# A side-by-side input projection with pre-scaled operands and a shorter weight lead, in a two-layer trunk kernel

## The chip, the cores and the metric

The kernel runs on one core of a Trainium2 chip. The metric is the time of one launch in device microseconds (us). A core has engines that run side by side, each through its own list of instructions in order: TensorE (PE; its weight loads are shown as PEld), VectorE (DVE), ScalarE (ACT), GpSimd (POOL) and SyncE (SP, which issues the large transfers).

## The reference

A trunk of two layers over 256 tokens of width 2048: a Mamba-2 mixer and an FFN, then an attention mixer and an FFN. The change touches only the input of the first mixer:

```python
h = rms_norm(x, mix_norm[layer])
proj = h @ w_in
z = proj[..., :SSM_D_INNER]
xbc = proj[..., SSM_D_INNER:SSM_D_INNER + SSM_CONV_DIM]
dt_raw = proj[..., SSM_D_INNER + SSM_CONV_DIM:]
xbc = jax.nn.silu(causal_depthwise_conv(xbc, conv_w, conv_b))
...
y = ssd_chunked(xs * dt[..., None], dt * a, b_in, c_in)
y = y + xs * d_skip[:, None]
y = y.reshape(bsz, seq, SSM_D_INNER) * jax.nn.silu(z)
y = rms_norm(y.reshape(bsz, seq, SSM_N_GROUPS, group), norm_w.reshape(SSM_N_GROUPS, group))
```

`w_in` has 4096 columns of z, 4096 of x, 1024 each of B and C and 64 of dt, all float32.

## The kernel before

All weights lie in HBM as one list of 128x2048 tiles in the order of use. Each tile is loaded by SyncE into one of three buffers `w` and used as two halves of 128x1024. For each half `split` (L145) issues a ScalarE cast to a high part `wh` and a VectorE subtraction that leaves the low part `wl`. Activations, too, are kept as a high and a low part, one beside the other in an operand of a `slot`. A product is the sum of high times high, high times low and low times high. `next_half` (L160) keeps the splits ahead of TensorE by `AHEAD` halves, and `wh` and `wl` have one buffer more than that, so a split waits until TensorE has freed the buffer of an earlier half.

There are two schemes for the three products. `t_units` (L222) makes them with three matmuls of 256 columns (L240). `p_unit` (L250) makes the two that share the high weights with one matmul of 512 columns (L261: high and low operand side by side, into two halves of a bank) and the third with one of 256 (L265); the two halves of the bank have to be added afterwards (`joined`, L270). The FFNs and half of the output projections use `p_unit`; the input projection uses `t_unit`, for each of 8 groups `g` one unit of 256 columns (B and C), one of 512 (x) and one of 512 (z), and in group 0 one of 128 (dt). That is 20 halves in a group, and 2 of dt.

A unit sums in one of two accumulators `acc`. `begin_unit` (L199) lets a unit start only when the sums of the unit before the last have been read (the key `("evac", u)` is done).

Everything else is background: generators in queues, which put out one step at each `yield`. After each half `bg.step()` goes through the queues and takes one step of each, as long as the work put out, counted in estimated us of VectorE and ScalarE, leaves a debt under 0.75 of a half's `SHARE` (1.3 and 1.4). `bg.need(key)` takes steps of all queues, whatever the debt, until the key is done:

```python
    def step(self, free=False):
        self.debt = [max(d - s, -1.4) for d, s in zip(self.debt, self.SHARE)]
        for q in self.queues:
            if free or all(d < 0.75 * s for d, s in zip(self.debt, self.SHARE)):
                self.advance(q)

    def need(self, key):
        while key not in self.done:
...
            for q in self.queues:
                self.advance(q)
```

The operand of the input projection is x times its gain, without the norm's factor `rb` (a row over the tokens), which needs sums over all of x (`prep`, L377). The factor is multiplied into the sums as they are read (`scaled`, L392). After that a group's B, C and x go through a convolution (`first_tap` on ScalarE, three `taps` on VectorE), a tanh and a `gate`; `ssd` (L532) makes the group's scan with decay rows fetched by GpSimd's queue, and `ssd_norm` (L610) the operand of the output projection.

## Time and profile before

| | |
|---|---|
| median of 3 runs | 2698.09 us (2697.56 to 2698.7) |
| the profiled execution, its own time | 2698.51 us |
| its span, first to last instruction | 2696.4 us |
| TensorE busy | 2673.5 us (99%) |
| VectorE busy | 1700.7 us (63%) |
| ScalarE busy | 1326.3 us (49%) |
| mean granted TensorE clock | 0.999 |

The input projection runs from about 11 to about 550 us, the output projection follows, the first FFN is from about 700 to 1380 us, the attention layer follows, and the second FFN ends the program. A busy share says little by itself here: what counts is what TensorE waits for, and where.

### The profile page before, as it was taken

What the parts mean: (1) busy time and instruction counts of PE and PEld (TensorE: products, weight loads), DVE (VectorE), ACT (ScalarE), POOL (GpSimd) and SP (SyncE); (2) the same over time, 40 slices, a digit from 0 to 9 for tenths busy, and PEclk for the clock granted to TensorE, in tenths of its full rate; (3) what the DMA queues carried; (4) which work ended last, traced back from release to release, by engine and by line L of the source; (5) the groups of instructions that cost most, each with busy time, mean ns of one, the idle gap of its engine ahead of it and who ended that gap; (6) DMA issues with size and microseconds to landing.
All of it is one profiled execution on the core that took longest, in us unless ns stands there. A gap on an engine that the chain in (4) does not pass through costs nothing.

```text
span 2696.4 us, 40315 instructions
## 1 busy us (share of the span) xinstructions
PE 2673.5 (99%) x16460; PEld 2391.9 (89%) x16460; DVE 1700.7 (63%) x2104; ACT 1326.3 (49%) x1947; POOL 199.8 (7%) x215
## 2 busy tenths in 40 slices
PE   7999999999999999999999999999999999999999
PEld 7999999999888888888888888888888888888888
DVE  6777777756566666665555777766666666665444
ACT  5666666654454444444444555544454444444332
POOL 1011111110000000000001330220000000000000
PEclk9999999999999999999999999999999999999999
DMA  5454555545555555555555554553455555555553
GB/s 222 178 184 175 187 179 189 177 177 187 188 188 188 188 188 187 189 189 193 190 189 203 183 186 152 185 185 141 156 188 188 188 188 188 188 188 194 197 198 128
DMA packets 71432, 495.75 MB, mean 184 GB/s; under 512 B 8320, under 2 KB 8704, under 8 KB 13008
## 3 DMA queue, kind: packets, MB, share of 16 engines
q1 hardware_dynamic: 68400, 483.81, 49.5%
q0 software_dynamic: 2848, 9.37, 1.1%
q8 instruction: 129, 2.11, 0.3%
q14 instruction: 55, 0.45, 0.1%
HBM read 490.99 MB, written 2.16 MB: 183 GB/s over the span
## 4 chain that ended last, share of the span: by engine, by line
PE 98%; ACT 1%; issue 0%; DVE 0%; POOL 0%; DMA 0%; SPq 0%; ACTq 0%; POOLq 0%
PE acc L261 39%; PE acc L240 21%; PE acc L265 20%; PE acc L217 15%; PE bg L588 1%; PE bg L754 0%; PE bg L787 0%; PE bg L860 0%; PE bg L549 0%; ACT wh L38 0%; ACT slot L38 0%; PE bg L324 0%; PE bg L784 0%; PE bg L862 0%; DMA xres<-in_x_dram 0%
## 5 line engine op out<-in xcount | busy, mean ns | idle before, releaser
L38 DVE TENSOR_TENSOR wl<-w,wh 128x1024 fp32r<-128x1024 f32 x914 | 1128.3, 1236 | 904.7 <-ACT wh L38 903.7
L38 ACT CAST wh<-w 128x1024 fp32r<-128x1024 f32 x914 | 955.5, 1047 | 1089.8 <-PE acc L261 507.2
L261 PE MATMUL acc<-slot,wh 128*128 128x512 f32 x4416 | 1106.7, 392 | 2.1 <-DVE xres L38 1.7
L261 PEld LDWEIGHTS acc<-slot,wh 128*128 128x128 f32 x4416 | 794.2, 189 | 145.1 <-issue 2.7
L265 PEld LDWEIGHTS acc<-slot,wl 128*128 128x128 f32 x4416 | 602.4, 190 | 43.0
L265 PE MATMUL acc<-slot,wl 128*128 128x256 f32 x4416 | 615.7, 282 | 0.0
L240 PE MATMUL acc<-slot,wh 128*128 128x256 f32 x3232 | 430.1, 286 | 12.8 <-ACT wh L38 10.7
L240 PEld LDWEIGHTS acc<-slot,wh 128*128 128x128 f32 x3232 | 404.8, 193 | 19.9 <-ACT wh L38 10.8
L217 PE MATMUL acc<-wh,slot 128*128 128x512 f32 x1152 | 290.5, 394 | 0.0
L217 PEld LDWEIGHTS acc<-wh,slot 128*128 128x128 f32 x1152 | 213.7, 188 | 43.2
L240 PE MATMUL acc<-slot,wl 128*128 128x256 f32 x1616 | 226.8, 283 | 0.9 <-DVE wl L38 0.9
L240 PEld LDWEIGHTS acc<-slot,wl 128*128 128x128 f32 x1616 | 208.6, 192 | 1.1 <-DVE wl L38 1.1
L217 PE MATMUL acc<-wl,slot 128*128 128x512 f32 x576 | 154.2, 389 | 0.0
L217 PEld LDWEIGHTS acc<-wl,slot 128*128 128x128 f32 x576 | 108.1, 188 | 22.7
L38 ACT ACTIVATE tmp<-tmp 128x256 f32<-128x256 f32 (+1 forms) x104 | 46.8, 450 | 163.9 <-DVE tmp L38 163.6
L284 POOL TENSOR_TENSOR tmp<-tmp 128x256 f32<-128x256 f32 x32 | 27.6, 868 | 1022.1 <-ACT tmp L38 1017.0
L38 ACT ACTIVATE wide<-tmp,bias 128x128 f32<-128x128 f32 x192 | 62.9, 391 | 13.9 <-PE bg L588 9.4
L38 DVE SCALAR_TENSOR_TENSOR slot<-tmp,vec,slot 128x255 f32<-128x255 f32 (+1 forms) x144 | 67.6, 528 | 0.0
L38 DVE TENSOR_TENSOR tmp<-tmp 128x256 f32<-128x256 f32 x88 | 37.4, 425 | 42.6 <-ACT tmp L38 42.6
L38 DVE TENSOR_TENSOR tmp<-acc,tmp 128x512 f32<-128x512 f32 x88 | 60.1, 683 | 4.0 <-ACT tmp L38 4.0
L38 DVE TENSOR_TENSOR tmp<-tmp,rb 128x512 f32<-128x512 f32 x88 | 60.3, 686 | 0.1
L38 ACT ACTIVATE tmp<-slot 128x128 f32<-128x128 f32 (+1 forms) x136 | 52.7, 394 | 14.9 <-DVE slot L38 13.8
(131 smaller groups left out, 1191.3 us busy)
## 6 DMA issues: line engine op xcount, KB each, us to landing
w<-in_weights_dram SPq DMA_DIRECT2D x455, 1024.0 KB, 4.8
tmp<-acum POOLq DMA_DIRECT2D x32, 256.0 KB, 4.6
xres<-in_x_dram SPq DMA_DIRECT2D x4, 512.0 KB, 7.8
w<-in_weights_dram SPq DMA_DIRECT2D x4, 512.0 KB, 8.4
out_dram<-xres SPq DMA_DIRECT2D x8, 256.0 KB, 2.2
slot<-in_mask_dram POOLq DMA_DIRECT2D x1, 384.0 KB, 5.6
slot<-in_q_norm_dram POOLq DMA_DIRECT2D x1, 192.0 KB, 5.6
slot<-in_k_norm_dram POOLq DMA_DIRECT2D x1, 192.0 KB, 7.5
```

The costliest lines, as they stand in the source:

```text
L38: return call(out, *args, **kw)
L217: T.matmul(ps[tb], X[k][:, part, tb * P:(tb + 1) * P], w[:, k % 2, :], start=(k == 0 and i == 0), stop=(k == 15 and i == 2))
L240: T.matmul(pss[j][:, b, c, :], w[:, k % kk, m * P:(m + 1) * P], X[k][:, part, :], start=(k == 0 and i == 0 and c == 0), stop=(k == nk - 1 ...
L261: T.matmul(ps[:, m], h[:, k % 4, m * P:(m + 1) * P], X[k], start=(k == 0), stop=False, skip_group_check=True)
L265: T.matmul(ps[:, m, 0], l[:, k % 4, m * P:(m + 1) * P], X[k][:, 0, :], start=False, stop=(k == nk - 1), skip_group_check=True)
L284: G.tensor_tensor(sq[:, 0, :], sq[:, 0, :], sq[:, 1, :], OP.add)
L588: T.matmul(o[:, tb * P:], xdt[:, tb, q * 64:(q + 1) * 64], m[:, 256 * tb:256 + 128 * tb], start=(tb == 0 and q % 4 < 2), stop=(tb == 1), s ...
```

## The change

- `p_unit` takes the place of `t_unit` for all of the input projection but dt. The units of x and z are cut into two of 256 columns each, in the order x, z, x, z, and the weights are laid out in that order.
- From group 1 on the operand is x times gain times `rb`, made once by the new generator `normed` in queue 1 behind `prep`. Group 0 still uses the operand without `rb` and multiplies its sums.
- `total` reads the sums: a ScalarE copy of one half of the bank, a VectorE add of the other. The sums of z and of B and C go straight into their final slot. dt is copied out before `rb` is there.
- The reading of z, B and C stands in a queue of its own, number 3; there are four queues. `prep` moves from queue 0 to queue 1.
- `AHEAD` goes from 3 to 2, `wh` and `wl` from four buffers to three. `tmp` has 8 buffers, and the decay rows get a ring `rows` of 2.
- `ssd_norm` uses the slot of z for its squares.

```diff
...
     def tmp(shape, dt=F32):
-        return small.tile(shape, dt, tag="tmp", bufs=6, name=name("tmp"))
+        return small.tile(shape, dt, tag="tmp", bufs=8, name=name("tmp"))
+
+    def rows(shape):
+        return small.tile(shape, F32, tag="rows", bufs=2, name=name("rows"))
 
     def wide():
         return small.tile([P, 384], F32, tag="wide", bufs=4, name=name("wide"))
@@ -128,13 +131,13 @@
     def bg_bank():
         return psum.tile([P, 512], F32, tag="bg", bufs=4, name=name("bg"))
 
-    bg = Background(3, (V, A))
+    bg = Background(4, (V, A))
 
 
     n_tiles = weights.shape[0]
     raw_tiles, ready = {}, deque()
     state = dict(issued=0, split=0, used=0)
-    AHEAD = 3
+    AHEAD = 2
 
     def issue():
         j = state["issued"]
@@ -148,8 +151,8 @@
         while state["issued"] <= min(i // 2 + 2, n_tiles - 1):
             issue()
         t = raw_tiles[i // 2][:, (i % 2) * 1024:(i % 2 + 1) * 1024]
-        h = wpool.tile([P, 1024], F32R, tag="wh", bufs=4, name=name("wh"))
-        l = wpool.tile([P, 1024], F32R, tag="wl", bufs=4, name=name("wl"))
+        h = wpool.tile([P, 1024], F32R, tag="wh", bufs=3, name=name("wh"))
+        l = wpool.tile([P, 1024], F32R, tag="wl", bufs=3, name=name("wl"))
         A.copy(h, t)
         V.tensor_tensor(l, t, h.bitcast(F32), OP.subtract)
         if i % 2:
@@ -247,7 +250,7 @@
     def t_unit(ncols, X, xkey, evac, q=0):
         t_units([(0, range(16))], ncols, 16, X, xkey, [evac], q)
 
-    def p_unit(nk, X, xkey, evac):
+    def p_unit(nk, X, xkey, evac, q=0):
 
 
         u, ps = begin_unit()
@@ -264,8 +267,8 @@
                 for m in range(2):
                     T.matmul(ps[:, m, 0], l[:, k % 4, m * P:(m + 1) * P], X[k][:, 0, :], start=False,
                              stop=(k == nk - 1), skip_group_check=True)
-            bg.step()
-        bg.add(0, evac(ps, u))
+            bg.step(units[0] == 1)
+        bg.add(q, evac(ps, u))
 
     def joined(ps):
 
@@ -388,18 +391,47 @@
         V.tensor_scalar(hpar[64:128, 1:2], hpar[64:128, 1:2], -1.0, None, OP.mult)
         V.memset(hpar[0:64, 1:2], 1.0)
         bg.done.add("prep")
-
-    def scaled(sums):
-        u = tmp([P, 2, S])
-        V.tensor_tensor(u, sums, rb[:, None, :].to_broadcast([P, 2, S]), OP.mult)
-        return u
+        bg.add(1, normed())
+
+    XN = {}
+
+    def normed():
+
+        vs, ts = {}, {}
+        for j in range(10):
+            if j >= 2:
+                v, t = vs.pop(j - 2), ts.pop(j - 2)
+                V.tensor_tensor(t[:, :, 1, :], v, t[:, :, 0, :].bitcast(F32), OP.subtract)
+                store(XN, 2 * (j - 2), t)
+                bg.done.add(("XN", j - 2))
+            if 1 <= j < 9:
+                ts[j - 1] = operand()
+                A.copy(ts[j - 1][:, :, 0, :], vs[j - 1])
+            if j < 8:
+                v = vs[j] = tmp([P, 2, S])
+                for i in range(2):
+                    k = 2 * j + i
+                    V.scalar_tensor_tensor(v[:, i, :], xt[:, k, :], gains[:, k:k + 1], rb, OP.mult, OP.mult)
+            yield
+
+    def total(ps, u, g, v):
+        A.copy(v, ps[:, :, 1])
+        yield
+        V.tensor_tensor(v, ps[:, :, 0], v, OP.add)
+        bg.done.add(("evac", u))
+        if g == 0:
+            while "prep" not in bg.done:
+                yield
+            V.tensor_tensor(v, v, rb[:, None, :].to_broadcast([P, 2, S]), OP.mult)
+        yield
 
     def dt_evac(ps, u):
+        xb, e, r, q = (wide()[:, 0:S] for _ in range(4))
+        A.copy(xb, ps[:, 0, 0])
+        bg.done.add(("evac", u))
         while "prep" not in bg.done:
             yield
-        xb, e, r, q = (wide()[:, 0:S] for _ in range(4))
-        V.tensor_tensor(xb, ps[:, 0, 0], rb, OP.mult)
-        bg.done.add(("evac", u))
+        V.tensor_tensor(xb, xb, rb, OP.mult)
         A.activation(xb, xb, AF.Identity, bias=hpar[:, 0:1])
         A.activation(e, xb, AF.Abs)
         A.activation(e, e, AF.Exp, scale=-1.0)
@@ -455,78 +487,58 @@
                 V.scalar_tensor_tensor(dst[:, m, d:], u[:, m, :S - d], cwb[:, j * 48 + ct:j * 48 + ct + 1],
                                        dst[:, m, d:], OP.mult, OP.add)
 
...
     def gate(out_, th, v):
         V.scalar_tensor_tensor(out_, th, 1.0, v, OP.add, OP.mult)
 
+    def conv(u, dst, cts):
+        first_tap(u, dst, cts)
+        yield
+        taps(u, dst, cts, (2, 1))
+        yield
+        taps(u, dst, cts, (0,))
+        yield
+        A.activation(u, dst, AF.Tanh)
+        yield
+        gate(dst, u, dst)
+
     def bc_evac(g):
         def gen(ps, u):
...
+            both = slot([P, 1024])
+            bc, v = (both[:, i:i + 512].rearrange("p (a t) -> p a t", t=S) for i in (0, 512))
+            yield from total(ps, u, g, v)
+            yield from conv(v, bc, (32 + g, 40 + g))
             BC[g] = bc, both[:, 512:896]
             yield
         return gen
 
-    def x_evac(g):
+    def x_evac(g, i):
         def gen(ps, u):
...
+            v = tmp([P, 2, S])
+            yield from total(ps, u, g, v)
+            if i == 0:
+                XS[g] = slot([P, 4, S])
+            yield from conv(v, XS[g][:, 2 * i:2 * i + 2, :], (4 * g + 2 * i, 4 * g + 2 * i + 1))
+            if i == 1:
+                bg.add(2, ssd(g))
+            yield
         return gen
 
-    def z_evac(g):
+    def z_evac(g, i):
         def gen(ps, u):
...
+            if i == 0:
+                sz[g] = slot([P, 4, S])
+            z = sz[g][:, 2 * i:2 * i + 2, :]
+            yield from total(ps, u, g, z)
+            th = tmp([P, 2, S])
+            A.activation(th, z, AF.Tanh, scale=0.5)
+            yield
+            gate(z, th, z)
+            if i == 1:
+                SZ[g] = sz.pop(g)
+            yield
         return gen
 
+    sz = {}
     BC, XS, SZ, Y = {}, {}, {}, {}
 
     def ssd(g):
...
-            ac[pair] = tmp([P, 2, S])
+            ac[pair] = rows([P, 2, S])
             h = 8 * g + 2 * pair
...
-            sz = SZ[g] if b == 0 else SZ.pop(g)
+            sz = SZ[g]
...
-        bg.add(1, ssd_norm(g, xs))
-
-    def ssd_norm(g, xs):
-        sq = [tmp([P, 2, S]) for _ in range(2)]
+        bg.add(1, ssd_norm(g, xs, SZ.pop(g)))
+
+    def ssd_norm(g, xs, sq):
+        sq = [sq[:, 0:2, :], sq[:, 2:4, :]]
         for b in range(2):
             A.activation(sq[b], xs[:, 2 * b:2 * b + 2, :], AF.Square)
         yield
@@ -630,17 +642,21 @@
             store(Y, 4 * g + 2 * i, t)
             bg.done.add(("Y", 2 * g + i))
 
-    bg.add(0, prep())
+    bg.add(1, prep())
     bg.need(("XT", 1))
     for g in range(NG):
-        t_unit(256, XT, "XT", bc_evac(g))
+        X, key = (XT, "XT") if g == 0 else (XN, "XN")
+        p_unit(16, X, key, bc_evac(g), 3)
         if g == 0:
             t_unit(128, XT, "XT", dt_evac, 2)
-        t_unit(512, XT, "XT", x_evac(g))
-        t_unit(512, XT, "XT", z_evac(g))
-    bg.need("rstd")
+        for i in range(2):
+            p_unit(16, X, key, x_evac(g, i))
+            p_unit(16, X, key, z_evac(g, i), 3)
+        if g == 0:
+            XT.clear()
     bg.need(("evac", units[0] - 1))
     clear_norm()
+    XN.clear()
     t_units(OUT0, 512, 32, Y, "Y", [t_residual(nb, 32) for nb in (0, 1)])
     for pair in range(4, 8):
         p_unit(32, Y, "Y", p_residual(pair, 32))
@@ -919,8 +935,9 @@
         put(r16, (w_in, 8192 + g * P, P), (w_in, 9216 + g * P, P))
         if g == 0:
             put(r16, (w_in, 10240, 64), (w_in, 10240, 64))
-        put(r16, (w_in, 4096 + g * 512, 512))
-        put(r16, (w_in, g * 512, 512))
+        for i in range(2):
+            put(r16, (w_in, 4096 + g * 512 + i * 256, 256))
+            put(r16, (w_in, g * 512 + i * 256, 256))
 
     def put_out(w, order, nk):
         for j, ks in order:
```

The built programs show how the instructions move on an engine. Names are those of the program: `wl` the low part of a weight half, `acc` an accumulator, `bg` a bank of the background work, `wide` and `tmp` scratch, `slot` a large buffer.

VectorE in group 0, before, around the reading of x (`tmp<-acc,rb`), with the softplus steps of dt (`wide`) between:

```order
L38 TENSOR_TENSOR wl_617<-w_486,wh_616 128x1024
L38 SCALAR_TENSOR_TENSOR wide_379<-wide_379,wide_378 128x256 x2
L38 TENSOR_TENSOR wl_648<-w_486,wh_647 128x1024
L38 TENSOR_TENSOR tmp_676<-acc_384,rb 128x512
L38 SCALAR_TENSOR_TENSOR wide_379<-wide_379,wide_378 128x256 x2
L38 TENSOR_TENSOR wl_683<-w_548,wh_682 128x1024
L38 TENSOR_TENSOR tmp_712<-acc_384,rb 128x512
L38 SCALAR_TENSOR_TENSOR wide_379<-wide_379,wide_377 128x256
L38 TENSOR_SCALAR wide_376<-wide_376 128x256
L38 SCALAR_TENSOR_TENSOR wide_379<-wide_379,wide_376 128x256
L38 TENSOR_SCALAR wide_379<-wide_379,vec 128x256
L38 TENSOR_TENSOR wl_719<-w_548,wh_718 128x1024
```

The same engine after, the last rows ahead of the unit z1 of group 0; `slot_713<-acc_443` is the sum of the unit z0:

```order
L38 TENSOR_TENSOR slot_697<-tmp_685,slot_697 128x2x256
L38 SCALAR_TENSOR_TENSOR wide_333<-wide_333,wide_332 128x256 x2
L38 SCALAR_TENSOR_TENSOR slot_335<-slot_335 128x512
L38 SCALAR_TENSOR_TENSOR wide_333<-wide_333,wide_331 128x256
L38 TENSOR_SCALAR wide_330<-wide_330 128x256
L38 SCALAR_TENSOR_TENSOR wide_333<-wide_333,wide_330 128x256
L38 TENSOR_SCALAR wide_333<-wide_333,vec 128x256
L38 SCALAR_TENSOR_TENSOR slot_539<-tmp_653,slot_539 128x512
L38 TENSOR_TENSOR slot_713<-acc_443,slot_713 128x512
L38 TENSOR_TENSOR slot_713<-slot_713,rb 128x512
L38 TENSOR_TENSOR wl_725<-w_549,wh_724 128x1024
L38 TENSOR_TENSOR wl_745<-w_549,wh_744 128x1024
```

Before, a wl stands after every one to four rows; after, the rows from `wl_633` (22 rows ahead of these) to `wl_725` hold no wl, and the sum stands second to last among them.

VectorE in group 1, before, while x of group 1 is multiplied and the scan of group 0 runs (`wide`):

```order
L38 TENSOR_TENSOR wide_1235<-wide_1235,slot_449 128x384
L38 TENSOR_TENSOR wl_1281<-w_1118,wh_1280 128x1024
L38 SCALAR_TENSOR_TENSOR slot_1148<-tmp_1270,slot_1148 128x512
L38 TENSOR_TENSOR wide_1273<-wide_1273,slot_449 128x384
L38 TENSOR_TENSOR wl_1320<-w_1118,wh_1319 128x1024
L38 TENSOR_TENSOR wide_1314<-wide_1314,slot_449 128x384
L38 TENSOR_TENSOR wl_1356<-w_1197,wh_1355 128x1024
L38 TENSOR_TENSOR wide_1348<-wide_1348,slot_449 128x384
L38 TENSOR_TENSOR wl_1396<-w_1197,wh_1395 128x1024
L38 TENSOR_TENSOR tmp_1424<-acc_1082,rb 128x512
L38 TENSOR_TENSOR wide_1389<-wide_1389,slot_449 128x384
```

The same engine after, the rows ahead of the unit z1 of group 1; `slot_1295<-acc_1056` is the sum of the unit z0:

```order
L38 TENSOR_TENSOR wide_1245<-wide_1245,slot_335 128x384
L38 SCALAR_TENSOR_TENSOR slot_1043<-slot_1043,vec 128x253 x2
L38 TENSOR_TENSOR wide_1260<-wide_1260,slot_335 128x384
L38 TENSOR_TENSOR tmp_1267<-acc_1141,tmp_1267 128x512
L38 TENSOR_TENSOR wide_1270<-wide_1270,slot_335 128x384
L38 SCALAR_TENSOR_TENSOR slot_1043<-slot_1043 128x512
L38 TENSOR_TENSOR wide_1283<-wide_1283,slot_335 128x384
L38 SCALAR_TENSOR_TENSOR slot_539<-slot_539,vec,bg_1228 128x256 x2
L38 SCALAR_TENSOR_TENSOR slot_1032<-tmp_1267,vec,slot_1032 128x255 x2
L38 SCALAR_TENSOR_TENSOR slot_1032<-tmp_1267,vec,slot_1032 128x254 x2
L38 TENSOR_TENSOR slot_1295<-acc_1056,slot_1295 128x512
L38 TENSOR_TENSOR wl_1310<-w_1142,wh_1309 128x1024
```

Here too a wl stood after every one to three rows, and now none stands ahead of `wl_1310` among those shown. The last one before is `wl_1207`, the eighth in a row; six rows lie between it and the first row shown (two taps of each kind, two `wide` and a gate).

TensorE at the start, before, from the end of the dt unit to the x unit (`acc_384`); L311 and L324 are the two matmuls of the norm:

```order
L240 MATMUL acc_294<-slot_246,wl_296 128x256 x2
L240 MATMUL acc_294<-slot_251,wl_296 128x256 x2
L311 MATMUL bg_359<-ones,rb 128x2 x2
L324 MATMUL bg_367<-tmp_364,ones 128x256
L240 MATMUL acc_384<-slot_101,wh_301 128x256 x16
L240 MATMUL acc_384<-slot_101,wl_302 128x256 x8
L240 MATMUL acc_384<-slot_106,wh_329 128x256 x16
```

TensorE at the same place after (the line numbers are 3 higher; `acc_340` is the first x unit):

```order
L243 MATMUL acc_262<-slot_227,wl_264 128x256 x2
L314 MATMUL bg_327<-ones,rb 128x2 x2
L264 MATMUL acc_340<-slot_101,wh_269 128x512 x4
L264 MATMUL acc_340<-slot_106,wh_269 128x512 x4
L268 MATMUL acc_340<-slot_101,wl_270 128x256 x4
L268 MATMUL acc_340<-slot_106,wl_270 128x256 x4
L264 MATMUL acc_340<-slot_140,wh_297 128x512 x4
L264 MATMUL acc_340<-slot_145,wh_297 128x512 x4
L268 MATMUL acc_340<-slot_140,wl_298 128x256 x4
L268 MATMUL acc_340<-slot_145,wl_298 128x256 x4
L327 MATMUL bg_386<-tmp_363,ones 128x256
```

The second matmul of the norm, L324, has moved from ahead of the x unit to behind its second half.

## Rows read from the trace of the kernel before

**Rows 1.** Stretches: us from:to, length, busy us (x instructions), PEclk, DMA share, GB/s.
```profile
0.00:70.00 70.00, 53.90 (x407) 52.48 (x408) 49.06 (x77) 37.44 (x57) 9.85 (x17) 0.95 0.58 216
...
135.00:270.00 135.00, 135.00 (x1123) 131.20 (x1122) 104.21 (x152) 84.99 (x142) 23.17 (x25) 1.00 0.50 179
...
700.00:1000.00 300.00, 300.00 (x1720) 264.04 (x1719) 184.52 (x216) 142.91 (x188) 3.60 (x5) 1.00 0.52 186
```

The five busy columns are PE, PEld, DVE, ACT and POOL.

**Rows 2.** Time order of TensorE where the schemes meet: start us, us, instructions merged.
```profile
629.85 2.08 PE L240 MATMUL acc<-slot,wh 128*128 128x256 f32 x16
631.77 1.12 PE L240 MATMUL acc<-slot,wl 128*128 128x256 f32 x8
632.73 2.00 PE L261 MATMUL acc<-slot,wh 128*128 128x512 f32 x8
634.57 1.11 PE L265 MATMUL acc<-slot,wl 128*128 128x256 f32 x8
635.52 2.00 PE L261 MATMUL acc<-slot,wh 128*128 128x512 f32 x8
```

**Rows 3.** Time order of TensorE at the start; in brackets the idle time before.
```profile
31.72 0.51 PE L311 MATMUL bg<-ones,rb 128*128 128x2 f32 x4
34.57 1.22 PE L324 MATMUL bg<-tmp,ones 128*128 128x256 f32 x2 [2.35 <-POOL tmp L321]
37.56 3.75 PE L240 MATMUL acc<-slot,wh 128*128 128x256 f32 x16 [1.77 <-DVE tmp L38]
...
42.11 2.08 PE L240 MATMUL acc<-slot,wh 128*128 128x256 f32 x16
...
73.79 2.08 PE L240 MATMUL acc<-slot,wh 128*128 128x256 f32 x16
```

**Rows 4.** Time order of VectorE in the same stretch.
```profile
32.26 0.16 DVE L38 TENSOR_SCALAR rstd<-bg 128x2 f32<-128x2 f32 x1 [1.39 <-PE bg L311]
...
36.72 0.69 DVE L38 TENSOR_TENSOR tmp<-acc,rb 128x512 f32<-128x512 f32 x1
```

**Rows 5.** Stretches as in rows 1, behind the idle time of rows 3.
```profile
37.56:39.00 1.44, 1.44 (x7) 1.44 (x8) 0.18 (x1) 1.16 (x3) 0.00 (x0) 0.50 0.00 0
...
41.00:42.00 1.00, 1.00 (x10) 1.00 (x10) 1.00 (x2) 0.72 (x2) 0.00 (x0) 0.89 0.00 0
```

**Rows 6.** Time order of three engines in group 1 of the projection.
```profile
99.29 1.05 ACT L38 CAST wh<-w 128x1024 fp32r<-128x1024 f32 x1 [2.57 <-PE acc L240]
99.99 2.08 PE L240 MATMUL acc<-slot,wh 128*128 128x256 f32 x16
100.37 1.23 DVE L38 TENSOR_TENSOR wl<-w,wh 128x1024 fp32r<-128x1024 f32 x1 [0.99 <-ACT wh L38]
...
111.60 0.87 PE L588 MATMUL bg<-wide,slot 128*64 128x256 f32 x8
```

**Rows 7.** Groups of instructions: xcount, busy us, mean ns of one, idle before.
```profile
L38 DVE TENSOR_TENSOR tmp<-acc,tmp 128x512 f32<-128x512 f32 x88 | 60.1, 683 | 4.0 <-ACT tmp L38 4.0
L38 ACT COPY tmp<-acc 128x512 f32<-128x512 f32 x88 | 51.0, 580 | 5.3 <-PE acc L265 5.3
...
L38 DVE TENSOR_TENSOR wide<-wide,slot 128x384 f32<-128x384 f32 x64 | 35.2, 550 | 0.0
...
L38 DVE SCALAR_TENSOR_TENSOR slot<-tmp,vec,slot 128x254 f32<-128x254 f32 x48 | 26.5, 593 | 0.0
...
L38 DVE SCALAR_TENSOR_TENSOR slot<-tmp,vec,slot 128x253 f32<-128x253 f32 x48 | 22.3, 505 | 0.0
L38 DVE SCALAR_TENSOR_TENSOR slot<-tmp,vec,slot 128x255 f32<-128x255 f32 x48 | 21.4, 485 | 0.0
...
L38 DVE SCALAR_TENSOR_TENSOR slot<-tmp,slot 128x512 f32<-128x512 f32 x24 | 16.4, 683 | 0.0
...
L38 ACT ACTIVATE wide<-tmp,bias 128x128 f32<-128x128 f32 x192 | 62.9, 391 | 13.9 <-PE bg L588 9.4 <-DMA tmp<-acum 4.4
...
L38 DVE SCALAR_TENSOR_TENSOR wide<-wide,wide 128x256 f32<-128x256 f32 x10 | 4.2, 422 | 0.2
```

More of the change, by code (lines that the diff above doesn't have):

```diff
@@ L456, in taps @@
                                        dst[:, m, d:], OP.mult, OP.add)
-    def half_tanh(v, scale):
-        th = tmp([P, 2, S])
-        A.activation(th, v, AF.Tanh, scale=scale)
-        return th
     def gate(out_, th, v):
         V.scalar_tensor_tensor(out_, th, 1.0, v, OP.add, OP.mult)
+    def conv(u, dst, cts):
[8 more added lines that the diff above has]
+        gate(dst, u, dst)
     def bc_evac(g):
         def gen(ps, u):
-            v = scaled(ps[:, :, 0])
-            bg.done.add(("evac", u))
-            yield
-            both, cts = slot([P, 1024]), (32 + g, 40 + g)
-            bc = both[:, 0:512].rearrange("p (a t) -> p a t", t=S)
-            first_tap(v, bc, cts)
-            yield
-            taps(v, bc, cts, (2, 1))
-            yield
-            taps(v, bc, cts, (0,))
-            yield
-            th = half_tanh(bc, 1.0)
-            yield
-            gate(bc, th, bc)
+            both = slot([P, 1024])
+            bc, v = (both[:, i:i + 512].rearrange("p (a t) -> p a t", t=S) for i in (0, 512))
+            yield from total(ps, u, g, v)
+            yield from conv(v, bc, (32 + g, 40 + g))
             BC[g] = bc, both[:, 512:896]
@@ L484, in bc_evac, with gen @@
         return gen
[L486 removed]
+    def x_evac(g, i):
         def gen(ps, u):
[L488 to L495 removed]
+            v = tmp([P, 2, S])
[5 more added lines that the diff above has]
+                bg.add(2, ssd(g))
+            yield
+        return gen
+    def z_evac(g, i):
+        def gen(ps, u):
+            if i == 0:
[4 more added lines that the diff above has]
+            A.activation(th, z, AF.Tanh, scale=0.5)
             yield
[L497 to L498 removed]
+            gate(z, th, z)
+            if i == 1:
+                SZ[g] = sz.pop(g)
             yield
[L500 to L528 removed]
+        return gen
+    sz = {}
     BC, XS, SZ, Y = {}, {}, {}, {}
```

35 lines of the change are left out of this document (removed).

## The prediction

> **What bounds the kernel now.** I read the stretches first [rows 1]: TensorE is busy for the whole of the projection's stretch (135 to 270 us) and of the first FFN's (700 to 1000 us), at the full clock; the first 70 us hold 16 us of its idle time. So the time is TensorE's own list of matmuls, and whatever holds that list up. Then I read the time-ordered rows at the border of the two matmul schemes [rows 2], which give the price of the new scheme directly; then the start [rows 3, 4, 5]; then how early the split weights are ready [rows 6]; then the durations of the background steps [rows 7]. I call the work on one 128x1024 weight half a half. A half of the separate scheme is 24 matmuls of 256 columns and takes 631.77 - 629.85 + 0.96 = 2.88 us from start to start; a half of the side-by-side scheme is 8 of 512 and 8 of 256 and takes 635.52 - 632.73 = 2.79 us [rows 2].
>
> **Part 1, the matmul scheme.** The projection has 20 halves in each of 8 groups, 160 in all (the two dt halves stay as they were). They go from 2.88 to 2.79 us: 160 x 0.087 = 13.9 us off TensorE's list. VectorE and ScalarE are not on the path for this, as long as they keep up.
>
> The Trainium skill (TensorE: Matmul & The Clock Gate, section "Wait — 56ns, not 53.3ns?") puts the fixed cost of one matmul at full clock at about 2.5 ns. The side-by-side scheme saves one matmul of three at equal columns, 1280 in all, so by the page's figure the gain would be an estimated 3.2 us and the sum below 11 us higher; the trace does not agree (8 matmuls fewer make a half 0.087 us shorter, 11 ns each), and I take the trace.
>
> **Part 2, the start.** Before, the third unit (x of group 0) waits for the first unit's sums, which are multiplied by rb before their bank is free; rb needs the norm. TensorE ends L311 at 32.2 us and starts the x unit at 37.56 us, and the two matmuls between are slow [rows 3]. Then the clock stands at 0.50 until about 41 us [rows 5] and the first 16 matmuls take 3.75 us instead of 2.08, a loss of 1.7 us. After, the sums are copied and added without rb, so the x unit needs only row rstd (32.26 + 0.16 us [rows 4]) and one 128x512 add of 0.68 us behind it: it starts at about 33.2 us, 4.3 us earlier, and the clock loss should mostly go. Gain up to here 6 us.
>
> **Part 3, what is added to VectorE and ScalarE.** Per unit of 256 columns: one more ScalarE copy (0.58 us [rows 7]), and the multiplication by rb becomes an add of the same size (0.68). Once, in group 0: 16 products and 8 subtractions for the normalised operands, 16 x 0.42 + 8 x 0.68 = 12.2 us of VectorE, beside 8 casts on ScalarE. Spread out this would be hidden: VectorE has 135 - 104 = 31 us free in 135 us of the projection [rows 1].
>
> **Part 4, the order, which decides.** It is not spread out. The planner hands out background steps after each half only while its debt is under 0.75 of a half's share; `need` hands them out from all queues, whatever the debt, until the wanted step is out. The z and B/C sums now stand in a queue of their own, one whole unit behind the other, and the unit after next cannot start before its bank's sum is out. With the 12 us of normalised operands in the debt the planner gives nothing out for 8 halves, then the next `need` drains every queue at once. The built order shows it: eight wl in a row, then a run of background steps with no wl among them, the awaited add as the last but one or last. There are 12 such runs, from z1 of group 0 to z1 of group 4, each at a unit whose wanted sum is of z or B/C; from group 5 on steps and wl alternate again.
>
> What one costs: let T be the end of the half before the unit. TensorE can do nothing after T until the awaited add is done, and VectorE works its list in order. How early can it begin the run? In the trace the subtraction of a later half starts 0.38 us after a half's start and takes 1.23 us [rows 6]; the last wl ahead of the run belongs to the unit's second half, so with a lead of two it is done at T - 2.79 + 0.38 + 1.23 = T - 1.2. ScalarE is free at about T - 2.4 by the same count. So TensorE waits for the VectorE rows of the run, less 1.2 us, or for the ScalarE rows less 2.4 if these are longer.
>
> The run at z1 of group 1 (the second place shown above): 12 taps, 4 of each length, 4 x (0.485 + 0.593 + 0.505) = 6.3; 6 products of 384 at 0.55 = 3.3; 2 gates and 2 adds at 0.68 = 2.7; 2 skip terms priced as a tap, 1.0. Together 13.3 us [rows 7], a wait of 12.1. The eleven runs after the first, priced in this way: VectorE 7.2, 13.3, 5.9, 7.9, 15.1, 4.7, 9.7, 12.0, 5.9, 4.3, 6.6 us, ScalarE longer only in the tenth (8.9, mainly its 128x128 rows at 62.9/192 = 0.33 each [rows 7]). Waits: 6.0 + 12.1 + 4.7 + 6.7 + 13.9 + 3.5 + 8.5 + 10.8 + 4.7 + 6.5 + 5.4 = 82.8 us. Within a run VectorE also waits now and then for ScalarE; following the shown run step by step costs 0.45 us more, so 11 x 0.45 = 5. In these waits TensorE does the background matmuls which before stood between its halves: about 5.3 us a group (four times L588, 0.8 each [rows 6], and 2 us of smaller ones), of which 17 us fall in the waits of the four groups. 82.8 + 5 - 17 = 71 us.
>
> The first run, z1 of group 0, has 3 gates, 5 subtractions and 3 adds or products at 0.68, 12 taps (6.3), 6 operand products and 15 softplus steps at 0.42: 7.5 + 6.3 + 8.9 = 22.7 us. VectorE comes to it late: from 33.2 us TensorE needs 12 halves, to T = 67.3 us (with 0.6 for the two matmuls of the norm), and VectorE is behind. rb comes out two halves and a small matmul after 33.2, at about 39.8 us; the wl ahead of the rb work waits for the buffer of the third half, 42.2, and ends at 43.4. From there 8 wl (9.9 us) and 14.4 us of other rows, priced as above, lead up to the run, which so begins at 67.7 us. So the half after the run starts at 67.7 + 22.7 = 90.4 us. Before, that half starts at 73.79 us [rows 3]. Net loss 16.6 us, the gain of the start already in it.
>
> Each wait also lets the clock fall. In the trace 2.35 us of idle were enough for slow matmuls right behind, and the x unit then lost 1.7 us [rows 3, 5]. 12 x 1.7 = 20 us; bounds 5 (only waits over 10 us count) and 25.
>
> **Part 5, three buffers and a lead of two elsewhere.** The lead over TensorE shrinks by one half, 2.79 us: a wl is then done 1.6 us after the start of a half and needed two halves later, behind 1.85 us of the hi matmuls, about 5.8 us of slack. Outside the projection the background rows between two wl are at most about 4 us in attention and under 2 in the FFNs, where VectorE is busy 185 of 300 us [rows 1]. I price it at 0; the upper bound is a rival. The own ring for decay rows: their transfers are issued 10 us or more ahead of their first reader, 0.
>
> **The sum**, against the profiled execution of 2698.5 us (its span is 2696.4; the median of the runs is 2698.1, 0.4 lower): 2698.5 + 16.6 + 71 + 20 - 142 x 0.087 (12.4, the halves after the first run) = 2794 us. Low end with the clock at 5, no extra waits and the first run 10 us shorter: 2764. High end with the longer clock bound and 25 us of dependency waits: 2825.
>
> **Rivals.** (a) Covered runs: the awaited sum comes out early in a run, and TensorE works on its two split halves, 5.6 us, through the rest. Then each wait is shorter by 5.6: 0.4 + 6.5 + 1.1 + 8.3 + 2.9 + 5.2 + 0.9 = 25, the first 11, clock on five waits 8.5, less 12.4: 2731 us. Against it: the add stands at the end of the run. (b) The other side: VectorE and ScalarE get through the runs while TensorE is still busy, which holds if they reach each run more than 10 us ahead of T, that is if they are not held by TensorE freeing weight buffers. Then only the gains are left, 2698.5 - 13.9 - 6.0 = 2679 us, faster. For it: VectorE is free a quarter of the projection [rows 1]. Against: a subtraction starts right after a half's start [rows 6], so the lead is set by the buffers, not by VectorE. (c) The shorter lead also bites outside: 60 steps of attention with 3 us or more of VectorE between two wl cost 1 us each, 2794 + 60 = 2854 us.
>
> **How the numbers follow.** Forecast 0.78, (a) 0.07, (b) 0.08, (c) 0.07. I predict 2794 us. The range 2728 to 2840 takes in the forecast's bounds and (a), and leaves out (b) and most of (c). What this kernel's measurement can tell from no change is about 0.2%, 5 us. Faster 0.08, same 0.01, slower 0.91.
>
> **What would show it.** Right: idle time of TensorE before the side-by-side matmuls, put down to VectorE's add into a slot, in about 12 gaps between 65 and 400 us, the longest 20 us or more near 70; the granted clock at 0.5 behind them; halves of 2.79 us between; the x unit's first matmul near 33 us; nothing changed from 700 us on. Wrong: TensorE without gaps there, gaps of the length of a run less 5.6 us, or new idle time in attention and the FFNs.

## The result and the profile after

The changed kernel takes 2765.65 us, the median of 4 runs (2762.99 to 2767.5), beside 2698.39 us for the kernel before (2697.56 to 2698.85) on the same chip: 1.0249 times as long, 95% interval 1.0237 to 1.0261. That is slower by 67 us. The profiled execution took 2762.99 us (span 2761.2), 64.5 us more than that of before.

Stretches of the kernel after, with the columns of [rows 1]:

```profile
70.00:135.00 65.00, 46.09 (x258) 40.04 (x259) 42.75 (x73) 27.81 (x45) 2.42 (x4) 0.87 0.33 119
135.00:270.00 135.00, 116.95 (x635) 95.99 (x633) 84.48 (x123) 72.30 (x128) 16.91 (x19) 0.92 0.45 154
...
700.00:1000.00 300.00, 300.00 (x1722) 264.08 (x1721) 183.40 (x211) 142.12 (x182) 7.02 (x10) 1.00 0.52 187
```

TensorE, busy for all of 135 to 270 us before, is now idle for 18 of these 135 us, and the mean granted clock there is 0.92 instead of 1.00. From 700 to 1000 us TensorE is busy for the whole stretch, as in [rows 1]. Nothing is lost behind the output projection's first sums either: the first add of a sum to `xres` starts at 693.2 us (628.4 before) and the last at 2757.3 (2692.5 before), 2064.1 us later in both. What TensorE waited for in the whole program (engine, tile and line <- releaser: us in total, times, longest):

```profile
PE bg L457 <- DVE wide L38: 18.7, 1, 18.7
PE bg L600 <- DVE wide L38: 14.9, 12, 2.0
PE bg L314 <- POOL slot L628: 13.1, 3, 9.1
PE acc L264 <- ACT wh L38: 10.5, 1, 10.5
PE acc L264 <- DVE slot L38: 7.6, 6, 3.0
PE acc L264 <- DVE tmp L38: 4.9, 4, 3.3
```

The fourth row is the first weights at the start, as before. In the first three, 46.7 us, a background matmul (`bg`) waits. Only in the last two, 12.5 us, does a half of a unit wait for a sum.

TensorE at the start and at the first gap, in order of time, the answer to [rows 3]:

```profile
32.56 2.11 PE L264 MATMUL acc<-slot,wh 128*128 128x512 f32 x8
...
35.46 2.00 PE L264 MATMUL acc<-slot,wh 128*128 128x512 f32 x8
...
65.67 1.11 PE L268 MATMUL acc<-slot,wl 128*128 128x256 f32 x8
85.49 0.69 PE L457 MATMUL bg<-cm,wide 128*128 128x128 f32 x2 [18.72 <-DVE wide L38]
85.83 3.20 PE L264 MATMUL acc<-slot,wh 128*128 128x512 f32 x8
```

VectorE beside that gap:

```profile
65.88 1.22 DVE L38 TENSOR_TENSOR wl<-w,wh 128x1024 fp32r<-128x1024 f32 x1
67.02 0.69 DVE L38 SCALAR_TENSOR_TENSOR slot<-tmp,slot 128x512 f32<-128x512 f32 x1
67.62 0.69 DVE L38 TENSOR_TENSOR slot<-tmp,slot 128x512 fp32r<-128x512 f32 x1
...
73.66 1.66 DVE L38 SCALAR_TENSOR_TENSOR slot<-slot,vec 128x255 f32<-128x255 f32 x4
...
85.09 0.35 DVE L38 TENSOR_SCALAR wide<-wide,vec 128x256 f32<-128x256 f32 x1
85.36 0.68 DVE L38 SCALAR_TENSOR_TENSOR slot<-tmp,slot 128x512 f32<-128x512 f32 x1
85.96 0.68 DVE L38 TENSOR_TENSOR slot<-acc,slot 128x512 f32<-128x512 f32 x1
```

The x unit starts at 32.56 us, and its second half at 35.46 where it was 42.11 [rows 3]. TensorE ends its half at 66.6 us, VectorE begins the long run at 67.0 and ends it at 86.6. The row to look at is the last one: the add `slot<-acc` that the planner had waited for runs at 85.96, and the unit behind it in the program had begun at 85.83. TensorE waited for `wide`, written at 85.09 and read by the background matmul L457, the entry ahead of the unit in its own list. The unit itself, z1, needs only the accumulator of the unit x1: the built program gives both the same banks, and the sum of x1 was out at 70.5 us. The wanted sum, that of z0, frees the accumulator of the unit after z1.

The gap at z1 of group 1 shows the same (TensorE rows and one VectorE row, the last):

```profile
149.86 1.52 PE L600 MATMUL bg<-wide,slot 128*64 128x256 f32 x16
...
158.60 1.54 PE L600 MATMUL bg<-wide,slot 128*64 128x256 f32 x6 [0.84 <-DVE wide L38]
160.08 3.61 PE L264 MATMUL acc<-slot,wh 128*128 128x512 f32 x8
161.85 0.68 DVE L38 TENSOR_TENSOR slot<-acc,slot 128x512 f32<-128x512 f32 x1
```

TensorE goes through the run's background matmuls one by one as VectorE's products come out, and again the unit starts ahead of the add. Its first eight matmuls take 3.61 us instead of 2.00. Two stretches at this place, first the slow half, then what follows:

```profile
160.08:163.70 3.62, 3.62 (x11) 2.93 (x11) 3.59 (x5) 0.28 (x1) 0.78 (x1) 0.55 0.00 0
163.70:165.50 1.80, 1.80 (x13) 1.63 (x13) 0.70 (x1) 1.05 (x1) 0.00 (x0) 1.00 0.00 0
```

Behind 10 us in which TensorE was busy for 5.4 (150 to 160 us) the granted clock is 0.55, near the lower of its two levels, 1.2 GHz, for about a half; then it is 2.4 GHz again.

At the gap before, the unit z0 of group 1, no background matmul stands in front (one TensorE row, one VectorE row):

```profile
127.37 2.06 PE L264 MATMUL acc<-slot,wh 128*128 128x512 f32 x8 [3.25 <-DVE tmp L38]
130.30 0.69 DVE L38 TENSOR_TENSOR slot<-acc,slot 128x512 f32<-128x512 f32 x1
```

Here the unit waits for the sum of x (`tmp`), and starts 2.9 us before the awaited add. In all, nine of the twelve delayed units start before the awaited add has ended, by 0.3 to 5.6 us. The other three, at 190.46, 270.73 and 355.06 us, start 0.15 us after it.

### The profile page after: what moved, and what is told of

The parts are those of the page before. It is cut to its first block, busy times and chain, and to the rows that moved or that the text cites. A ratio compares the mean times of both kernels' runs of the same rounds, so it can differ in the third digit from the quotient of the medians.

```text
span 2761.2 us, 37728 instructions
## 1 busy us (share of the span) xinstructions
PE 2682.8 (97%) x15180; PEld 2337.1 (85%) x15180; DVE 1722.9 (62%) x2133; ACT 1350.1 (49%) x1996; POOL 203.8 (7%) x215
## 4 chain that ended last, share of the span: by engine, by line
PE 93%; DVE 3%; ACT 2%; issue 1%; DMA 0%; POOL 0%; SPq 0%; DVEq 0%; ACTq 0%; POOLq 0%
PE acc L264 48%; PE acc L268 24%; PE acc L220 14%; PE acc L243 4%; DVE slot L38 2%; DVE wl L38 1%; PE bg L600 1%; ACT wide L38 1%; ACT slot L38 0%; DVE wide L38 0%; PE bg L770 0%; PE bg L803 0%; PE bg L876 0%; ACT wh L38 0%; DVE tmp L38 0%
## 5 line engine op out<-in xcount | busy, mean ns | idle before, releaser
L264 PE MATMUL acc<-slot,wh 128*128 128x512 f32 x5696 | 1446.8, 396 | 25.6 <-ACT wh L38 10.5
L264 PEld LDWEIGHTS acc<-slot,wh 128*128 128x128 f32 x5696 | 1034.4, 191 | 219.3 <-issue 11.8
L268 PEld LDWEIGHTS acc<-slot,wl 128*128 128x128 f32 x5696 | 779.5, 191 | 56.5 <-DVE wl L38 0.3
L268 PE MATMUL acc<-slot,wl 128*128 128x256 f32 x5696 | 796.1, 283 | 0.0
L220 PEld LDWEIGHTS acc<-wl,slot 128*128 128x128 f32 x576 | 108.1, 188 | 22.7
L38 ACT ACTIVATE tmp<-tmp 128x256 f32<-128x256 f32 x88 | 36.8, 418 | 163.8 <-DVE tmp L38 163.8
L243 PE MATMUL acc<-slot,wh 128*128 128x256 f32 x672 | 88.5, 284 | 0.0
L243 PEld LDWEIGHTS acc<-slot,wh 128*128 128x128 f32 x672 | 83.7, 192 | 0.9 <-issue 0.7
L38 ACT COPY tmp<-acc 128x512 f32<-128x512 f32 x104 | 60.6, 583 | 23.0 <-PE acc L268 23.0
L38 ACT ACTIVATE wide<-rows,bias 128x128 f32<-128x128 f32 x192 | 62.9, 391 | 4.6 <-PE bg L600 4.3
L600 PE MATMUL bg<-wide,slot 128*64 128x128 f32 (+1 forms) x256 | 35.0, 360 | 14.9 <-DVE wide L38 14.9
L38 DVE SCALAR_TENSOR_TENSOR slot<-tmp,vec,slot 128x255 f32<-128x255 f32 (+2 forms) x96 | 49.2, 568 | 0.0
```

Of the source, the lines that this page charges most:

```text
L38: return call(out, *args, **kw)
L220: T.matmul(ps[tb], X[k][:, part, tb * P:(tb + 1) * P], w[:, k % 2, :], start=(k == 0 and i == 0), stop=(k == 15 and i == 2))
L243: T.matmul(pss[j][:, b, c, :], w[:, k % kk, m * P:(m + 1) * P], X[k][:, part, :], start=(k == 0 and i == 0 and c == 0), stop=(k == nk - 1 ...
L264: T.matmul(ps[:, m], h[:, k % 4, m * P:(m + 1) * P], X[k], start=(k == 0), stop=False, skip_group_check=True)
L268: T.matmul(ps[:, m, 0], l[:, k % 4, m * P:(m + 1) * P], X[k][:, 0, :], start=False, stop=(k == nk - 1), skip_group_check=True)
L600: T.matmul(o[:, tb * P:], xdt[:, tb, q * 64:(q + 1) * 64], m[:, 256 * tb:256 + 128 * tb], start=(tb == 0 and q % 4 < 2), stop=(tb == 1), s ...
```

## The experiments

The theory to be tested: TensorE loses what stands in the long runs, which the waits of the planner set off. Its rivals: the shorter lead, the added load on VectorE and ScalarE, the owed work of the normalised operands, the separate queue as such. Within the theory it was open what TensorE waits for in a run: the awaited add, or its own background matmuls.

**The lead and the buffers.** The kernel before with the change's lead and buffers alone:

```diff
-    AHEAD = 3
+    AHEAD = 2
-        h = wpool.tile([P, 1024], F32R, tag="wh", bufs=4, name=name("wh"))
-        l = wpool.tile([P, 1024], F32R, tag="wl", bufs=4, name=name("wl"))
+        h = wpool.tile([P, 1024], F32R, tag="wh", bufs=3, name=name("wh"))
+        l = wpool.tile([P, 1024], F32R, tag="wl", bufs=3, name=name("wl"))
```

> The kernel before with a lead of two and three buffers of wh and wl, nothing else. Theory of the runs (background steps held back for many halves and then put out at once; TensorE stands behind what is late in them): no runs here, so 2698 us, within 4. Rival of the lead (three buffers are what lets TensorE wait): at least 2740 us, with idle time of TensorE before weights. Rival of the load (the joined sums are more than VectorE and ScalarE can carry): 2698 us.

Measured 2699.6 us, 1.0005 times before (0.9995 to 1.0014): no difference. Then the other way, the changed kernel with the old lead, the space taken from the ring of the decay rows:

```diff
-        return small.tile(shape, dt, tag="tmp", bufs=8, name=name("tmp"))
+        return small.tile(shape, dt, tag="tmp", bufs=6, name=name("tmp"))
-        return small.tile(shape, F32, tag="rows", bufs=2, name=name("rows"))
+        return tmp(shape)
-    AHEAD = 2
+    AHEAD = 3
```

(and four buffers of `wh` and `wl`)

> The changed kernel with a lead of three and four buffers again (tmp back to 6 buffers, decay rows in them, to make room). The runs of background steps are the same as in the changed kernel, one half later. Theory of the runs: VectorE and ScalarE come to each run up to 2.8 us earlier, so each of the 12 waits is up to 2.8 us shorter, 20 to 35 us in all: 2728 to 2746 us, gaps at the same places. Rival of the lead: the gaps go, about 2680 us. Rival of the load: no change, 2763 to 2768 us.

Measured 2766.4 us, 1.0252 (1.0237 to 1.0267). The theory of the runs had expected a gain of 20 us or more, and there was none; this expectation was wrong. Its trace says why. TensorE's longest wait there; then VectorE's last subtraction ahead of the run at z1 of group 1, with TensorE around it; then the same subtraction in the changed kernel:

```profile
PE bg L457 <- DVE wide L38: 19.0, 1, 19.0
```

```profile
149.75 1.23 DVE L38 TENSOR_TENSOR wl<-w,wh 128x1024 fp32r<-128x1024 f32 x1 [1.57 <-ACT wh L38]
151.27 1.11 PE L268 MATMUL acc<-slot,wl 128*128 128x256 f32 x8
152.31 1.52 PE L600 MATMUL bg<-wide,slot 128*64 128x256 f32 x16
```

```profile
147.31 1.23 DVE L38 TENSOR_TENSOR wl<-w,wh 128x1024 fp32r<-128x1024 f32 x1 [1.57 <-ACT wh L38]
```

With a lead of three there is one more split ahead of the run, and that split waits for the same TensorE progress: it ends at 150.98, 1.3 us ahead of the end of TensorE's last half (152.3), as with a lead of two (148.54 against 149.8). VectorE begins the run no earlier, and the further half that lies ready can't be used, since L600 stands ahead of it.

**What is counted as owed work.** The changed kernel, in which the normalised operands of `normed` don't count in the planner's debt:

```diff
         for j in range(10):
+            used = V.used, A.used
...
+            V.used, A.used = used
             yield
```

> The changed kernel, but the planner doesn't count the normalised operands as debt; all work is still done. In the built order the first run has 16.8 us of VectorE rows instead of 23.8, and of the other eleven only three of 5.0, 3.7 and 6.3 us are left. Theory of the runs: the first wait about 12 us instead of 19, the others 8 us in all instead of 67 (of which some 17 were background matmuls done in them anyway), most of the clock's 14 us gone: about 2701 us (2692 to 2714). Rival of the lead: the lead is still two, 2750 us or more. Rival of the load: the same work in the same stretch, 2755 us or more.

Measured 2711.99 us, 1.0050 (1.0035 to 1.0065), inside the range. The planner no longer falls behind, and most of the later gaps are gone: TensorE is busy 508.4 of the 530 us from 70 to 600 (after: about 473). The largest wait left:

```profile
PE bg L459 <- DVE wide L38: 13.7, 1, 13.7
```

**The wait takes steps of one queue.** The changed kernel, in which the copies and adds of the sums go into a first queue of their own and their further steps into others, and a wait for a sum takes steps of the first alone:

```diff
     def need(self, key):
+        while self.first and key not in self.done and key[0] == "evac" and self.queues[0]:
+            self.advance(self.queues[0])
...
         V.tensor_tensor(v, ps[:, :, 0], v, OP.add)
         bg.done.add(("evac", u))
+        yield q
```

(a number given by a step moves the rest of its generator to that queue)

> The changed kernel, but the reading of the sums (copy, add) stands in a queue of its own ahead of all others, what follows goes to other queues, and the wait for a sum takes steps from that queue alone. Lead of two, three buffers, normalised operands and their debt as in the changed kernel. No run over 4.3 us of VectorE rows is left in the built order. Theory of the runs: all gaps go, and the gains stay: 160 halves x 0.087 = 13.9 and 6.7 at the start, 2698.4 - 20.6 = 2678 us (2673 to 2686). Rival of the lead: 2740 us or more. Rival of the load: 2750 us or more, with VectorE or ScalarE busy all through the projection.

Measured 2679.01 us (2678.97 to 2679.05), 0.9928 times before (0.9913 to 0.9943), inside the range. This version is faster than both kernels, by 19.4 us and 86.6 us. Its stretches from 70 us:

```profile
70.00:135.00 65.00, 65.00 (x378) 57.15 (x377) 54.02 (x84) 35.29 (x48) 1.87 (x3) 1.00 0.56 189
135.00:270.00 135.00, 135.00 (x807) 116.23 (x807) 111.79 (x169) 98.77 (x181) 19.82 (x24) 1.00 0.54 189
```

VectorE has the same work to do as in the changed kernel. In the second stretch it is even busier, 112 us against 84, as more of the projection falls into it, and TensorE has no gap. So the load is not the cause, and the whole loss lies in where the steps stand.

The same with less: the queue that holds the sum is advanced first, but the sums stay behind the convolutions of their own queue.

```diff
     def need(self, key):
+        mine = self.where.get(key)
+        while mine and key not in self.done:
...
+            self.advance(mine)
...
```

(and the other queues as before, if that one can't go on)

> The changed kernel, with the one difference that, while a unit waits for a sum, background steps are taken only from the queue that holds that sum, and from the others only if that one can't go on. VectorE's four longest runs that are left in the built order are estimated at 7.5, 6.5, 6.5 and 5.8 us, all others at 4.1 or less. Theory A (what costs is the length of VectorE's run that the wait sets off, by draining every queue): about 2685 us, 2678 to 2700, with the gaps on TensorE from 70 to 600 us nearly closed. Theory B (the separate serial queue, or the scaled operands' counting as owed work, costs by itself): 2705 to 2766.

Measured 2712.48 us, 1.0051 (1.0035 to 1.0068). That is in the range of theory B, and 12 us above the range of A. TensorE's two longest gaps, and between them one of another kind, with the VectorE row that ends it:

```profile
73.66 3.46 PE L272 MATMUL acc<-slot,wh 128*128 128x512 f32 x8 [6.59 <-DVE slot L38]
...
95.95 0.68 DVE L38 TENSOR_TENSOR slot<-tmp,slot 128x512 fp32r<-128x512 f32 x1
96.78 1.74 PE L272 MATMUL acc<-slot,wh 128*128 128x512 f32 x4 [2.83 <-DVE slot L38]
...
149.24 3.75 PE L272 MATMUL acc<-slot,wh 128*128 128x512 f32 x8 [5.58 <-DVE slot L38]
```

From 66 to 400 us there are nine gaps of 0.3 to 6.6 us, 21.5 us together, and the stretches 70:135 and 135:270 have a clock of 0.87 and 0.97, by estimate some 12 us more: that is about the 33 us above `sums`. In the two longest no background matmul stands ahead of the unit, and TensorE does wait for the add, at the end of two of the runs that I had counted as harmless. These cost about their length less a us, by the prediction's own rule for an add at the end. Three more gaps, 6.3 us, stand inside the first unit of group 1, which waits for its normalised operands (`slot<-tmp`): these come late here, which neither theory named. Draining all queues thus costs 53 us (2765.7 - 2712.5). The other 33 us (2712.5 - 2679.0) go with the place of the sums behind a convolution, as in the first half of theory B, and with the late operands; which share is whose was not measured apart.

**Another queue order.** The changed kernel with z, B and C read in the first queue, beside x:

```diff
-        p_unit(16, X, key, bc_evac(g), 3)
+        p_unit(16, X, key, bc_evac(g), 0)
...
-            p_unit(16, X, key, z_evac(g, i), 3)
+            p_unit(16, X, key, z_evac(g, i), 0)
```

> The changed kernel, with the one difference that reading z, B and C out of the projection is put back into the first background queue and has no queue of its own. In the built order VectorE's unbroken runs between two casts of projection weights no longer stand at three places a group but at nearly every unit of groups 0 to 5, and add up to about 200 us of VectorE work where the changed kernel has about 116. Theory A (TensorE loses what VectorE and GpSimd do in a run, because background matmuls that want that run's late outputs stand before the next half in TensorE's own order): slower than the changed kernel, 2800 us, 2780 to 2825. Theory B (the separate queue is itself the fault, and one queue is all that has to be restored): about 2680. If neither the queue nor the runs matter: 2766 as the changed kernel.

Measured 2831.25 us, 1.0497 (1.0473 to 1.0521), 6 us above the range of theory A and far from B's 2680. One queue for all sums is worse. TensorE's largest wait in total:

```profile
PE acc L264 <- DVE slot L38: 31.5, 18, 2.8
```

These are halves that wait for what VectorE writes to a slot, 18 times, so here theory A's background matmuls are only a part of the loss.

**The add alone, or TensorE's own list.** The experiment for the step of the prediction that the trace contradicts. The changed kernel, in which the queue that holds the sum is advanced until the sum is out, and then every other queue by as many steps:

```diff
+        mine = self.where.get(key)
+        rounds = 0
+        while mine and key not in self.done:
...
+            self.advance(mine)
+            rounds += 1
...
+        for _ in range(rounds):
+            for q in self.queues:
+                if q is not mine:
+                    self.advance(q)
```

> The changed kernel, with the one difference that, while a unit waits for a sum, the queue that holds the sum is advanced first until the sum is out, and only then every other queue by as many steps. In the built order the first long VectorE run, ahead of the unit z1 of group 0, keeps all of its rows (23.8 us as priced from the rows of before), but the awaited add stands 9.1 us into it instead of last; the background matmuls of that run still stand ahead of the unit in TensorE's order. The second run keeps its 7.2 us with the add 4.0 us into it; the later runs are gone. Theory A (TensorE stands behind the background matmuls of its own list, whose inputs come late in the run): the first gap stays at about 19 us although the sum is there after some 9; 2705 us, 2700 to 2709. Theory B (the rule of the prediction: TensorE waits for the awaited add alone): the first gap shrinks to about 8.5 us; 2693 us, 2689 to 2697.

Measured 2763.03 us, 1.0237 (1.0220 to 1.0255): the time of the changed kernel, in neither range. One thing in the expectation was false: the later runs are not gone. In the trace every run keeps its rows, and the awaited add starts 0.6 to 5.2 us into it instead of near its end. That makes the test a sharper one. If the add were what TensorE waits for, most of the loss would go; nothing went. VectorE, and TensorE at the first gap:

```profile
71.17 0.68 DVE L38 TENSOR_TENSOR slot<-acc,slot 128x512 f32<-128x512 f32 x1
...
87.11 0.35 DVE L38 TENSOR_SCALAR wide<-wide,vec 128x256 f32<-128x256 f32 x1
```

```profile
87.51 0.69 PE L473 MATMUL bg<-cm,wide 128*128 128x128 f32 x2 [20.98 <-DVE wide L38]
```

The sum is there at 71.85 us, and TensorE stands until 87.51 for the input of its background matmul. In the list of waits the halves' waits for a sum in a slot fall from 7.6 to 2.8 us, and those of the background products rise from 14.9 to 20.2:

```profile
PE bg L473 <- DVE wide L38: 21.0, 1, 21.0
PE bg L616 <- DVE wide L38: 20.2, 13, 4.8
```

**The gains, one by one.** The kernel before, with the start's order alone: the first group's dt, B and C are copied out ahead of `rb`, and `prep` goes into queue 1.

```diff
+        xb, e, r, q = (wide()[:, 0:S] for _ in range(4))
+        A.copy(xb, ps[:, 0, 0])
+        bg.done.add(("evac", u))
         while "prep" not in bg.done:
             yield
-        xb, e, r, q = (wide()[:, 0:S] for _ in range(4))
-        V.tensor_tensor(xb, ps[:, 0, 0], rb, OP.mult)
-        bg.done.add(("evac", u))
+        V.tensor_tensor(xb, xb, rb, OP.mult)
...
-    bg.add(0, prep())
+    bg.add(1, prep())
```

> The kernel before, in which only the order at the start differs: the dt and B/C products of the first group are copied out ahead of rb, and the preparation of that group goes behind them, so that TensorE's accumulator comes free before rb is there. Theory A (the time that the changed kernel's first x unit starts earlier, 6.7 us, is owed to this copy alone and is kept to the end): 2691.7 us, 2689 to 2694. Theory B (the start is won only together with the side-by-side scheme, or lost again at the next wait): 2698, within 1.5 us of the kernel before.

Measured 2692.46 us (2692.31 to 2692.75), 0.9978 (0.9969 to 0.9987): 6.0 us are won by the start alone, and kept. From here to `sums` there are 13.45 us; the side-by-side scheme was to bring 13.9. Last, `sums` without the operands that carry `rb`, every group multiplying its sums after the add:

```diff
-        bg.add(1, normed())
...
-        if g == 0:
+        if True:
             while "prep" not in bg.done:
                 yield
             V.tensor_tensor(v, v, rb[:, None, :].to_broadcast([P, 2, S]), OP.mult)
...
-        X, key = (XT, "XT") if g == 0 else (XN, "XN")
+        X, key = XT, "XT"
```

> The version called sums (a first queue for the copies and adds of the projection's sums alone), in which besides no scaled operand is made: every group multiplies by the plain transposed x, and VectorE multiplies each sum by rb after it, as the kernel before does. VectorE's runs stay at 4.3 us or less. Theory A (scaled operands give nothing by themselves; the gain is that of the projection scheme and of the earlier first sum): 2679 us, 2676 to 2684, the time of sums. Theory B (taking the multiplication by rb away from VectorE is part of the gain): 2690 or more.

Measured 2683.43 us, 0.9946 (0.9931 to 0.9961), at the upper end of theory A's range and 4.4 us above `sums`. The projection has no gap; the difference shows at the beginning of the output projection:

```profile
553.52 2.42 PE L248 MATMUL acc<-slot,wh 128*128 128x256 f32 x16 [2.44 <-ACT slot L38]
```

There operands of the output projection come late, 2.4 us here and 0.7 at another place, with slower matmuls behind. So the scaled operands give some 4 us at most, behind the projection. That the multiplications in the sums' path are what delays these operands is likely, and wasn't tested apart.

## Why the prediction was right, and where it was off

Predicted were 2794 us, measured 2765.65. The sign and the place held; the rule that set the length of the waits did not, and each of the three losses in the sum was priced 40 to 50% too high.

- **Part 1 and 2, the gains.** Halves of 2.79 us: shown, for example from 89.83 to 92.62 us. The x unit was put at 33.2 us and came at 32.56; gain of the start 6 us expected, 6.65 in the trace, 6.0 in `start`. Of the scheme's 13.9 us `sums` against `start` shows 13.45; the scaled operands have a share in that, and without them 9.0 us are left (`unscaled` against `start`).
- **Part 4, the runs.** Twelve gaps stand between 66 and 400 us, at the places named, the longest near 70; a small one that was not forecast, 1.5 us with a slow half behind it, ends at 460. That VectorE begins a run 1.2 us ahead of T held at z1 of group 1 (148.5 against 149.8); the first run, put at 67.7, began at 67.0.
- **The step that failed** is "TensorE can do nothing after T until the awaited add is done". The unit needs another accumulator than the one awaited in nine of the twelve gaps, and starts before that add has ended. What holds TensorE is its own list, in order: in seven gaps, the longest among them, background matmuls whose inputs the run makes late stand ahead of the unit. In three more it is the sum of x, which comes earlier in the run, and only in two, with 0.3 us at the end of a third, the awaited add itself. The sign that the prediction named, idle time put down to the add into a slot, is 7.6 of the 59.2 us of waits listed above without the first weights. `addfirst` shows it for the long gaps: the add early, the time the same. The false rule came near the right size by luck, because the add stood last in the run and the late background inputs not far ahead of it. It also led to rival (a) in a wrong form: not an early add would cover the runs, only the absence of late background matmuls in front of the unit. And it hid GpSimd: three waits of 13.1 us in all are for its sums for the norm, which the prediction doesn't have. Ahead of the longest of these, 9.1 us, GpSimd itself had waited 3.4 us for a VectorE row of the run.
- **The sizes.** The first run: net loss 16.6 us predicted, 12.0 measured (the unit at 85.83 instead of 73.79). The run began 0.7 us earlier, its rows took 19.6 us instead of 22.7, and the unit didn't wait for the last 0.8. The eleven other waits with their background matmuls taken off: 71 predicted, 50 measured (the delays of the units add up to about 67, less 17). The clock: 12 x 1.7 = 20 predicted, about 13 measured (nine slow first halves of 2.83 to 3.78 us in place of 2.00). With the 12.4 us of gains, 12 + 50 + 13 - 12.4 = 63, beside 64.5 measured.
- **Why the waits were priced too high.** For the eleven it is the false rule. Counted to the end of the awaited add, their delays would be 91 us, near the 88 (82.8 + 5) of the prediction; counted to the start of the unit they are 67. In the first run it is the adding of durations. Rows that follow each other overlap: at 67.02 and 67.62 two rows of 0.69 us start 0.60 apart, and four taps take 1.66 us together, 0.42 each, where the means of [rows 7] say 0.49 to 0.59. The durations of the run's rows add up to 22.2 us, near the 22.7 of the prediction, and the rows take 19.6.
- **The range.** Its high end, with 5 us more for the clock and 25 for dependency waits, adds up to 2824 us, not 2825.
- **Part 5, the shorter lead.** Priced at 0; `lead2` shows 0, and behind the projections the changed kernel takes the time of before. Rival (c) is out. Rival (b), gains only, is what `sums` made of the change: 2679 us predicted for it, 2679.0 measured.

## What to carry to other kernels

An engine that works its list in order stops at the first entry whose input is late, whatever lies ready behind it; so when a wait makes a planner put out work, ask what all of that work puts into the bottleneck engine's list ahead of the next unit, and let the wait put out no more than the step it waits for. That step should stand in a queue with nothing long ahead of it. Price a run of short instructions from start to start, not by adding durations.

## What the hardware showed

- **More lead bought nothing.** 2766.4 us with four weight buffers, 2765.65 with three, in this kernel: where each split is released by the consumer's progress, a further buffer adds a split and moves no start.
- **VectorE's taps have two prices.** Away from GpSimd four taps took 1.66 us, beside a GpSimd instruction 2.68:

```profile
159.25 2.68 DVE L38 SCALAR_TENSOR_TENSOR slot<-tmp,vec,slot 128x255 f32<-128x255 f32 x4
159.49 1.38 POOL L586 TENSOR_TENSOR slot<-slot,slot 128x512 f32<-128x512 f32 x1 [10.48 <-DVE slot L38]
```

The means of [rows 7] mix the two. The Trainium skill, in "GPSIMD Engine Reference", section "Specifications", says that GpSimd shares its way to SBUF with VectorE, and that VectorE instructions with two inputs in SBUF contend with it. The two rows agree, with 1.02 us added beside a GpSimd instruction of 1.38; no run here took GpSimd's work away.

- **A short gap left the clock alone, longer ones did not.** In `needone` the first eight matmuls behind 6.59 and 5.58 us of idle time took 3.46 and 3.75 us, at a granted clock of 0.56 (73.66 to 77.10 us) and 0.50 (149.24 to 153.00). Behind 0.74 us they took 2.09, at 1.00 (87.19 to 89.20):

```profile
87.19 2.09 PE L272 MATMUL acc<-slot,wh 128*128 128x512 f32 x8 [0.74 <-DVE tmp L38]
```
